# A fused encoder block on one core: seven-product jobs with a fourth raw buffer, splits placed where their target comes free, and wide closing weights

## The chip, the cores and the metric

The kernel runs on one core of one Trainium2 chip. The metric is the device time of one execution in microseconds (us). Engines are named as in the profile: PE is TensorE's matmul, PEld its weight load, DVE is VectorE, ACT is ScalarE, POOL is GpSimd, SP is the sync engine, which issues nearly all DMAs here.

## The reference

The program computes one block of an encoder over 512 frames of 1024 channels: a SwiGLU feed-forward, a mixer of two parallel branches, a second SwiGLU feed-forward, and a final normalisation.

```
def swiglu(h, w_in, w_out):
    a, b = jnp.split(h @ w_in, 2, axis=-1)
    return (jax.nn.silu(a) * b) @ w_out
...
    mod = (jax.nn.silu(c) @ w_ada[l] + b_ada[l]).reshape(B, 3, 3, 1024)
    h = modulate(rms_norm(x, g_ffn1[l]), mod[:, 0, 0], mod[:, 0, 1])
    x = x + 0.5 * mod[:, 0, 2][:, None, :] * swiglu(h, w_ffn1_in[l], w_ffn1_out[l])
    ...                                   # mixer: pooling branch and state-space branch
    h = modulate(rms_norm(x, g_ffn2[l]), mod[:, 2, 0], mod[:, 2, 1])
    x = x + 0.5 * mod[:, 2, 2][:, None, :] * swiglu(h, w_ffn2_in[l], w_ffn2_out[l])
return rms_norm(x, g_final)
```

The change lies in the second feed-forward: w_in is 1024 x 5632, w_out is 2816 x 1024. The 2816 gated channels are 22 blocks of 128, called f; the 1024 output channels are 8 blocks, called d.

## The kernel before

**Numbers as two halves.** All arithmetic is near full float32 precision: a matrix is split into a high half (a cast to the matmul's type, on ScalarE) and a low half (value minus high, a subtraction on VectorE). `put_split` (L262, L263) does this for activations, `split` (L1263, L1265) for weights. A product is then three matmuls: high x high, high x low, low x high (`mm3`, L257 to L259).

**Units.** The program is a list of units. A unit is one piece of weights (`src`), the matmuls that use it (`mm`), what comes before them (`pre`) and after them (`post`). One loop walks the list and issues everything; each engine then runs its own instructions in the order issued. Just before a unit's matmuls the loop calls `prefetch`, which issues splits and loads of later units: at position q, first all splits in `splits_at[q]`, then all loads in `loads_at[q]`. A plain unit is loaded 4 positions ahead (LA) into one of three `raw` buffers and split 2 ahead (SA) into one of three pairs of `wh` and `wl`. Units marked `late` prefetch behind their matmuls.

**The second feed-forward** (`ffn_seven`). In order:
- Eight steps, here g0 to g7, of the opening group (`group6`): step k multiplies 768 columns of weights with rows k of the normalised input, into six PSUM banks. The steps' `pre` also make the input: `make_h` for step k+1 (VectorE L215, ScalarE L219, VectorE L247, and on GpSimd an unsplit copy in HF, L221). When two steps' rows are there, `h_sums` forms four sums on GpSimd (L239 to L242), into two alternating 1024-column parts of MISC, and appends their split to `late_splits`. From k=4 on each `pre` first issues one of these. After g7, three gate stores (`gate_store`: silu, product, split).
- Two plain units, which give block f=3 (24 wide matmuls each; a third gate store pair's `post` issues late splits that are left).
- 36 jobs, numbered here 0 to 35, which give f=4 to 21. A job is a half of an inner dimension, computed as a seven-product scheme on 2 x 2 blocks of 256 frames. Jobs 4n and 4n+1 make the silu side of a pair of f's, 4n+2 and 4n+3 the other side. Each job has two units, here called 5a and 5b. The first unit (`mm1`) uses four weight blocks in `wh`/`wl`, 24 matmuls of 256 columns; the second (`mm2`) three blocks in one of four places of its own (J2A, J2A, J2B, and the second halves of HH and HL in even rows), 18 matmuls. After the first unit of an odd job `post1` forms sums of products inside PSUM: a copy on ScalarE (L547), four sums on VectorE (L548 to L551), a copy on ScalarE (L552). After the second unit of an odd job follows silu (`done_a`) or the gate product with its split (`done_b`).
- A job's four raw blocks are loaded into one of three raw buffers (two halves of MISC, and ADA); GpSimd then forms four more from them (L515 to L517). Both splits read the buffer. Order of units: 0a 1a, 2a 3a, 0b 1b, 4a 5a, 2b 3b, and so on.
- Outward units: three blocks of eight, each one d and six f's (18 wide matmuls), stand behind 4b 5b, 16b 17b and 28b 29b; the next job pair's first units follow. At the end the last four f's: four units of two f's ahead of and behind 34b 35b, four more of two f's, two of four f's, each with the residual, and the last two d's in `tail`, which runs them by halves of the frames so that the final norm can begin.
- `residual` (L634) adds to X on VectorE; for the last blocks ScalarE squares (L185) and scales (L646), and GpSimd adds the squares (L186).

Of the kernel before, what the change touches and what calls it, by code (L numbers as in the profile page):

```python
# [54 lines left out]
def block_kernel(ctx, tc, a, out):  # L55
# [175 lines left out]
    def h_sums(kp):  # L231
# [3 lines left out]
        o = 1024 * (kp % 2)  # L235
        t = MISC[:, o:o + 1024].rearrange("p (s t) -> p s t", s=4)
# [35 lines left out]
    def group6(s, src, post, pre0=None):  # L272
# [15 lines left out]
        for k in range(KT):  # L288
            def pre(k=k):
# [160 lines left out]
    def ffn_seven(s, w6, win, wout):  # L450


        JR = [MISC[:, 2048:4096], ADA, MISC[:, 0:2048]]
# [6 lines left out]
        def post6(pst):  # L460
            new_gslots()
            t1 = big("J2A", [P, 4096], F32R, "TB")
            t2 = big("J2B", [P, 2048], F32R, "MM")
            st8["p2"] = [(by256(t[:, o:o + 768]), by256(t[:, o + 768:o + 1536])) for t, o in ((t1, 0), (t1, 1536), (t2, 0))]

            st8["p2"].append((HH[:, 0:6:2, HB], HL[:, 0:6:2, HB]))
# [5 lines left out]
        def plain(f, ab, slot, hold):  # L472
# [13 lines left out]
            return Unit(win[ab], 1024, mm, None, post)  # L486
# [17 lines left out]
        def half_units(src, pr, kh, far):  # L504
# [3 lines left out]
            def load():  # L508
                t = JR[njob[0] % 3]
                job["n"], job["t"] = njob[0], t  # L510
                assert njob[0] < 3 or njob[0] - 3 in st8["free"]
                njob[0] += 1
                nc.sync.dma_start(out=t[:, 768:1792], in_=src)
                c = t.rearrange("p (i w) -> p i w", w=256)
# [4 lines left out]
            def split1():  # L519
# [24 lines left out]
            def post1():  # L544
                h1, h2 = slice(0, 256), slice(256, 512)
                e = ev()
                S.copy(out=e[:, h1], in_=pr.a[:, h1])  # L547
                V.tensor_tensor(out=e[:, h2], in0=pr.a[:, h2], in1=e[:, h1], op=ALU.add)  # L548
                V.tensor_tensor(out=e[:, h1], in0=pr.b[:, h1], in1=e[:, h2], op=ALU.add)
                V.tensor_tensor(out=pr.a[:, h2], in0=pr.b[:, h2], in1=e[:, h2], op=ALU.add)  # L550
                V.tensor_tensor(out=pr.b[:, h2], in0=pr.b[:, h2], in1=e[:, h1], op=ALU.add)  # L551
                S.copy(out=pr.b[:, h1], in_=e[:, h1])  # L552
# [11 lines left out]
            u1.load, u1.split, u1.lead, u1.far = load, split1, 3, far  # L564
            u2 = Unit(src, 768, mm2, None, pr.done if kh else None)
            u2.load, u2.split, u2.twin = (lambda: None), split2, u1
            return u1, u2

        def pair(n, slot):
# [10 lines left out]
            def done_b():  # L580
                two = lambda x: x.rearrange("p (f t) -> p f t", f=2)
                t, o, ol = (GHA, slot, GLA) if slot < 4 else (gslots["gc"], 0, None)
                for e, p, cs in zip(pa.s, (pb.a, pb.b), (HA, HB)):
                    g = ev()
                    V.tensor_tensor(out=g, in0=e, in1=p, op=ALU.mult)
# [4 lines left out]
                    put_split(hi, lo, two(g))  # L590
# [3 lines left out]
            for ab, pr in enumerate((pa, pb)):  # L594
                us = [half_units(win[2 + 4 * n + 2 * ab + kh], pr, kh, 6 if n else 4) for kh in range(2)]
# [3 lines left out]
        def out_unit(d, f0, f1, s0, hold, first=True, last=True, lastb=False):  # L599
            def mm(hi, lo):  # L600
                if first:
                    hold.append(ps())
                p = hold[0]
                for i in range(f1 - f0):
                    w = slice(i * P, (i + 1) * P)
                    mm3(p, hi[:, w], lo[:, w], *gslots[s0 + i], first and i == 0, last and i == f1 - f0 - 1)

            post = (lambda: residual(s, d, hold[0], lastb)) if last else None
            return Unit(wout[d, :, f0 * P:f1 * P], (f1 - f0) * P, mm, None, post)
# [8 lines left out]
        hold = [[] for _ in range(4)]  # L618
        for i in range(18):
# [612 lines left out]
    ffn_seven(2, a["w_f2_6"], a["w_f2_in"], a["w_f2_out"])  # L1232
# [5 lines left out]
    loads_at, splits_at = {}, {}  # L1238
    for j, i in enumerate(wunits):
        loads_at.setdefault(j - units[i].far, []).append(j)  # L1240
        t = units[i].twin
        splits_at.setdefault(j - units[i].lead if t is None else order[units.index(t)] - 1, []).append(j)
# [194 lines left out]
```

## Time and profile before

| | |
|---|---|
| median of 3 runs | 1090.03 us (1087.83 to 1090.41) |
| the profiled execution | 1087.91 us, span 1086.1 us, mean clock 0.987 |
| busy: PE, PEld | 1039.0 us (96%), 876.0 us (81%) |
| busy: DVE, ACT, POOL | 716.9 us (66%), 388.6 us (36%), 386.6 us (36%) |
| HBM | 126 GB/s over the span |

Rows of the profile read as follows. A timeline row has start, duration, engine, line, operation, output<-inputs, shapes, and in brackets the idle time before it with what ended it. Consecutive matmuls overlap, so their pace is read from start to start. A row of the waits has the total, the number and the longest. In rows of a list, three durations in ns are minimum, median and maximum; L263, for instance, is a helper's line and stands for all callers. The second feed-forward begins at about 690 us and runs to the end.

### The profile page before, as it was taken

To read this page: it belongs to the slowest core of one execution; us is meant where nothing else is said; L and a number is where in the kernel's file an instruction comes from. 1 tells how busy PE (TensorE), PEld (TensorE's weight loads), DVE (VectorE), ACT (ScalarE), POOL (GpSimd) and SP (SyncE) were. 2 spreads that over 40 slices of the span, in tenths; PEclk is the share of its full clock that TensorE was granted. 3 is DMA by queue.
4 is the path that set the end of the run, shared out by engine and by line. 5 is a ranking of instruction groups with operands and counts; after the bars stand their busy time and mean duration, and the time that the engine had idled before them with its cause. 6 is when DMAs were issued, how large, how long until landed. Compare 5 with 4: busy or idle time off the path is not lost.

```text
span 1086.1 us, 14290 instructions
## 1 busy us (share of the span) xinstructions
PE 1039.0 (96%) x5474; PEld 876.0 (81%) x5474; DVE 716.9 (66%) x1123; ACT 388.6 (36%) x589; POOL 386.6 (36%) x339
## 2 busy tenths in 40 slices
PE   9899999999999999989999999998999999999995
PEld 7678888888888888877888888977879888988874
DVE  6956878999796366789623474566636764675544
ACT  5242222222223243633343342344423542443343
POOL 2400100499885231234400001684433613562103
PEclk9999999999999999999999999998999999999998
DMA  9555554564474222222343322132232232323012
GB/s 351 196 208 199 196 194 159 203 220 168 165 243 177 65 80 77 94 68 78 105 137 107 97 97 83 44 101 84 84 131 78 79 126 87 99 102 132 35 54 88
DMA packets 46904, 138.24 MB, mean 127 GB/s; under 512 B 5218, under 2 KB 10466, under 8 KB 46835
## 3 DMA queue, kind: packets, MB, share of 16 engines
q1 hardware_dynamic: 46658, 136.73, 37.1%
q8 instruction: 43, 0.70, 0.3%
q0 software_dynamic: 176, 0.59, 0.1%
q14 instruction: 27, 0.21, 0.1%
HBM read 134.15 MB, written 3.15 MB: 126 GB/s over the span
## 4 chain that ended last, share of the span: by engine, by line
PE 68%; DVE 16%; ACT 5%; issue 4%; DMA 4%; POOL 2%; SPq 0%; DVEq 0%; ACTq 0%; POOLq 0%
PE ps L257 19%; PE ps L259 19%; PE ps L258 19%; PE ps L499 3%; DMA MISC<-w_f_in 2%; PE ps L282 2%; PE ps L283 1%; ACT wh L262 1%; PE ps L286 1%; DVE wl L1265 1%; DVE ev L693 1%; DVE J2A L263 1%; DVE ev L215 1%; DMA ADA<-w_f_in 1%; ACT wh L1263 1%
## 5 line engine op out<-in xcount | busy, mean ns | idle before, releaser
L1265 DVE TENSOR_TENSOR wl<-raw,wh 128x1024 fp32r<-128x1024 f32 (+4 forms) x157 | 182.3, 1167 | 89.5 <-ACT wh L1263 89.2
L259 PE MATMUL ps<-HH,wl 128*128 128x512 f32 (+1 forms) x544 | 212.0, 390 | 4.6 <-DVE wl L1265 4.6
L1263 ACT CAST wh<-raw 128x1024 fp32r<-128x1024 f32 (+4 forms) x171 | 151.3, 892 | 178.8 <-PE ps L258 88.2
L257 PE MATMUL ps<-HH,wh 128*128 128x512 f32 (+1 forms) x544 | 212.5, 391 | 0.0
L258 PE MATMUL ps<-HL,wh 128*128 128x512 f32 (+1 forms) x544 | 211.9, 389 | 0.0
L259 PEld LDWEIGHTS ps<-HH,wl 128*128 128x128 f32 x544 | 102.4, 188 | 29.0 <-DVE wl L1265 5.4
L257 PE MATMUL ps<-GHA,wh 128*128 128x512 f32 (+1 forms) x308 | 119.7, 389 | 6.1 <-ACT wh L1263 6.1
L257 PEld LDWEIGHTS ps<-HH,wh 128*128 128x128 f32 x544 | 102.4, 188 | 23.6 <-ACT PM L926 0.2
L258 PEld LDWEIGHTS ps<-HL,wh 128*128 128x128 f32 x544 | 102.3, 188 | 23.2
L259 PE MATMUL ps<-GHA,wl 128*128 128x512 f32 (+1 forms) x308 | 118.9, 386 | 1.2 <-DVE wl L1265 1.2
L258 PE MATMUL ps<-GLA,wh 128*128 128x512 f32 (+1 forms) x308 | 118.0, 383 | 0.0
L186 POOL TENSOR_TENSOR ACC<-ACC,ev 128x512 f32<-128x512 f32 x15 | 19.4, 1294 | 219.4 <-ACT ev L185 219.4
L634 DVE SCALAR_TENSOR_TENSOR X<-ps,MOD,X 128x512 f32<-128x512 f32 (+1 forms) x78 | 54.9, 705 | 61.1 <-PE ps L259 61.0
L515 POOL TENSOR_TENSOR MISC<-MISC 128x512 f32<-128x512 f32 x24 | 31.4, 1309 | 138.9 <-DMA MISC<-w_f_in 138.9
L132 DVE CUSTOM_DVE_ANT_0 ADA<-ADA,C,COL 128x1024 f32<-128x1024 f32 x50 | 74.8, 1496 | 0.0
L257 PEld LDWEIGHTS ps<-GHA,wh 128*128 128x128 f32 x308 | 57.8, 188 | 20.9 <-ACT wh L1263 8.8
L282 PE MATMUL ps<-HH,wh 128*128 128x512 f32 (+1 forms) x180 | 62.8, 363 | 8.8 <-ACT HH L219 8.8
L259 PEld LDWEIGHTS ps<-GHA,wl 128*128 128x128 f32 x308 | 57.8, 188 | 16.5 <-DVE wl L1265 4.1
L258 PEld LDWEIGHTS ps<-GLA,wh 128*128 128x128 f32 x308 | 57.8, 188 | 12.2 <-DVE GLA L263 0.2
L262 ACT CAST GHA<-ev 128x512 fp32r<-128x512 f32 x36 | 22.3, 621 | 121.3 <-DVE ev L406 76.3
L283 PE MATMUL ps<-HH,wl 128*128 128x512 f32 (+1 forms) x180 | 61.6, 356 | 0.5 <-DVE wl L1265 0.5
L499 PE MATMUL ps<-SH,wl 128*128 128x256 f32 x216 | 61.2, 283 | 0.0
(254 smaller groups left out, 2199.3 us busy)
## 6 DMA issues: line engine op xcount, KB each, us to landing
ADA<-w_ada SPq DMA_DIRECT2D x50, 512.0 KB, 3.6
raw<-w_f_in SPq DMA_DIRECT2D x40, 512.0 KB, 4.5
raw<-w_f_out SPq DMA_DIRECT2D x40, 384.0 KB, 3.6
MISC<-w_f_in SPq DMA_DIRECT2D x24, 512.0 KB, 3.5
raw<-w_in SPq DMA_DIRECT2D x18, 512.0 KB, 3.5
raw<-w_f SPq DMA_DIRECT2D x16, 384.0 KB, 3.7
ADA<-w_f_in SPq DMA_DIRECT2D x12, 512.0 KB, 3.5
raw<-w_f_out SPq DMA_DIRECT2D x16, 320.0 KB, 3.0
```

What stands on the lines that cost most here:

```text
L132: V.tensor_tensor_reduce(out=t, in0=t, in1=C, scale=1.0, scalar=bada[:, n:n + 1], op0=ALU.mult, op1=ALU.add, accum_out=MOD[:, n:n + 1],)
L257: E.matmul(pst, wh, xh, start=first, stop=False)
L258: E.matmul(pst, wh, xl, start=False, stop=False)
L259: E.matmul(pst, wl, xh, start=False, stop=last)
L262: S.copy(out=hi, in_=src)
L282: E.matmul(pst[m][:, cs], hi[:, w], xh, start=first, stop=False)
L283: E.matmul(pst[m][:, cs], lo[:, w], xh, start=False, stop=False)
L499: E.matmul(out_, w_[:, i, w], x_, start=first and n == 0, stop=last and n == 2, skip_group_check=True)
L515: G.tensor_tensor(out=c[:, 1:3], in0=c[:, 4:7:2], in1=c[:, 3:5], op=ALU.subtract)
L634: V.scalar_tensor_tensor(out=X[:, d, cs], in0=p[:, cs], scalar=MOD[:, s * 24 + 16 + d:s * 24 + 17 + d], in1=X[:, d, cs], op0=ALU.mult, op1 ...
L1263: S.copy(out=hi[:, 0:u.cols], in_=t)
L1265: eng.tensor_tensor(out=lo[:, 0:u.cols], in0=t, in1=hi[:, 0:u.cols].bitcast(F32), op=ALU.subtract)
```

## The change

- A fourth raw buffer: job n uses part n mod 4 of (first half of MISC, second half of MISC, MM, ADA). The sums of `h_sums` now go to four places in TB. The second units' four places are now TB, TB, the halves of HH and HL, and TB with C.
- Split and load positions are computed: a first unit or plain unit is split one position behind the third `wh` user before it, at most 4 ahead; a second unit one position behind the fourth second unit before it; a job is loaded where both splits of the job four before it are issued, jobs 0 to 3 at 7, 7, 7 and 5 positions ahead.
- The late splits leave the opening group and go, two each, to the `pre` of the two plain units.
- `post1`: all six instructions on VectorE. `done_b`: both products in place, then both casts, then both subtractions.
- The closing outward units, ten before, become three of 1024 columns (d 0 to 3 with f 18, 19; d 0 to 3 with f 20, 21; d 4, 5 with f 18 to 21), all behind 35b, with weights packed for them on the host.

Everything ahead of g3 is issued as before. The core of the diff:

```
@@ h_sums
-        o = 1024 * (kp % 2)
-        t = MISC[:, o:o + 1024].rearrange("p (s t) -> p s t", s=4)
+        t = TB.rearrange("p r q c -> p (r q c)")[:, 1024 * kp:1024 * kp + 1024].rearrange("p (s t) -> p s t", s=4)
@@ group6, pre
-                    if k >= 4 and late_splits:
-                        late_splits.pop(0)()
@@ plain
+            def pre():
+                for _ in range(2):
+                    late_splits.pop(0)()
             def post():
                 if ab:
                     gate_store(slot, hold[0], hold[1])
-                while late_splits:
-                    late_splits.pop(0)()
@@ half_units, load
-                t = JR[njob[0] % 3]
+                c = (MISC[:, 0:2048], MISC[:, 2048:4096], MM.rearrange("p q c -> p (q c)"), ADA)[n % 4]
@@ post1
-                S.copy(out=e[:, h1], in_=pr.a[:, h1])
-                V.tensor_tensor(out=e[:, h2], in0=pr.a[:, h2], in1=e[:, h1], op=ALU.add)
+                u2, u3 = e[:, h2], e[:, h1]
+                V.tensor_copy(out=u3, in_=pr.a[:, h1])
+                V.tensor_tensor(out=u2, in0=pr.a[:, h2], in1=u3, op=ALU.add)
...
-                S.copy(out=pr.b[:, h1], in_=e[:, h1])
+                V.tensor_copy(out=pr.b[:, h1], in_=u3)
@@ done_b
-                    g = ev()
-                    V.tensor_tensor(out=g, in0=e, in1=p, op=ALU.mult)
...
-                    put_split(hi, lo, two(g))
+                for e, p in zip(pa.s, (pb.a, pb.b)):
+                    V.tensor_tensor(out=e, in0=e, in1=p, op=ALU.mult)
+                for e, cs in zip(pa.s, (HA, HB)):
...
+                    S.copy(out=hi, in_=two(e))
+                    gs.append((hi, lo, two(e)))
+                for hi, lo, e in gs:
+                    V.tensor_tensor(out=lo, in0=e, in1=hi.bitcast(F32), op=ALU.subtract)
@@ end of ffn_seven
-        units.extend([out_unit(d, 18, 20, 0, hold[d], True, False) for d in range(2)])
         units.extend(seq[17][1])
-        units.extend([out_unit(d, 18, 20, 0, hold[d], True, False) for d in range(2, 4)])
-        units.extend([out_unit(d, 20, 22, 2, hold[d], False, True, True) for d in range(4)])
-        units.extend([out_unit(d, 18, 22, 0, [], lastb=True) for d in range(4, 6)])
+        hold = []
+        units.append(out_unit(range(4), 18, 20, 0, wend[0], hold, True, False))
+        units.append(out_unit(range(4), 20, 22, 2, wend[1], hold, False, True, True))
+        units.append(out_unit(range(4, 6), 18, 22, 0, wend[2], [], lastb=True))
@@ positions of splits and loads
-        loads_at.setdefault(j - units[i].far, []).append(j)
-        splits_at.setdefault(j - units[i].lead if t is None else order[units.index(t)] - 1, []).append(j)
+        if u.kind == 2:
+            split_at[j] = seconds[-4] + 1 if len(seconds) >= 4 else t - 1
...
+        split_at[j] = max(walls[-3] + 1, j - 4) if len(walls) >= 3 else j - SA
...
+            back = split_at[raws_of[-3]] if len(raws_of) >= 3 else -9
+            load_at[j] = max(split_at[j] - (3 if seconds else 2), back)
...
+        load_at[j] = max(split_at[seconds[n - 4]], split_at[jobs[n - 4]]) if n >= 4 else j - (7, 7, 7, 5)[n]
```

More of the change, by code (lines that the diff above doesn't have):

```diff
@@ L447, in ffn, with ffn_seven @@
         tail(s, wout[6, :, f0 * P:f1 * P], wout[7, :, f0 * P:f1 * P], f1 - f0, lambda k: gslots[k])
-    def ffn_seven(s, w6, win, wout):
-        JR = [MISC[:, 2048:4096], ADA, MISC[:, 0:2048]]
+    def ffn_seven(s, w6, win, wout, wend):
         st8 = {"free": set()}
@@ L461, in post6 @@
             new_gslots()
[L462 to L466, printed above, removed]
             for f in range(3):
@@ L502, in ffn_seven, with half_units @@
             pass
-        def half_units(src, pr, kh, far):
+        def half_units(src, pr, kh):
             job = {}
             def load():
-                t = JR[njob[0] % 3]
-                job["n"], job["t"] = njob[0], t
-                assert njob[0] < 3 or njob[0] - 3 in st8["free"]
+                n = njob[0]
+                assert n < 4 or n - 4 in st8["free"]
                 njob[0] += 1
-                nc.sync.dma_start(out=t[:, 768:1792], in_=src)
-                c = t.rearrange("p (i w) -> p i w", w=256)
+                c = (MISC[:, 0:2048], MISC[:, 2048:4096], MM.rearrange("p q c -> p (q c)"), ADA)[n % 4]
+                job["n"], job["t"] = n, by256(c)
+                nc.sync.dma_start(out=c[:, 768:1792], in_=src)
+                c = by256(c)
                 G.tensor_tensor(out=c[:, 1:3], in0=c[:, 4:7:2], in1=c[:, 3:5], op=ALU.subtract)
@@ L594, in pair, with out_unit, post @@
             for ab, pr in enumerate((pa, pb)):
-                us = [half_units(win[2 + 4 * n + 2 * ab + kh], pr, kh, 6 if n else 4) for kh in range(2)]
+                us = [half_units(win[2 + 4 * n + 2 * ab + kh], pr, kh) for kh in range(2)]
                 r.append(([u[0] for u in us], [u[1] for u in us]))
             return r
-        def out_unit(d, f0, f1, s0, hold, first=True, last=True, lastb=False):
+        def out_unit(ds, f0, f1, s0, src, hold, first=True, last=True, lastb=False):
+            nf = f1 - f0
             def mm(hi, lo):
                 if first:
[L602 to L609, printed above, removed]
+                    hold.extend(ps() for _ in ds)
+                for m, p in enumerate(hold):
+                    for i in range(nf):
+                        w = slice((m * nf + i) * P, (m * nf + i + 1) * P)
+                        mm3(p, hi[:, w], lo[:, w], *gslots[s0 + i], first and i == 0, last and i == nf - 1)
+            def post():
+                for d, p in zip(ds, hold):
+                    residual(s, d, p, lastb)
+            return Unit(src, len(ds) * nf * P, mm, None, post if last else None)
         hold = []
@@ L1236, in block_kernel @@
     order = {u: j for j, u in enumerate(wunits)}
-    loads_at, splits_at = {}, {}
-    for j, i in enumerate(wunits):
-        loads_at.setdefault(j - units[i].far, []).append(j)
-        t = units[i].twin
-        splits_at.setdefault(j - units[i].lead if t is None else order[units.index(t)] - 1, []).append(j)
+    wu = [units[i] for i in wunits]
+    split_at, load_at = {}, {}
+    walls, raws_of, jobs, seconds = [], [], [], []
+    for j, u in enumerate(wu):
+        if u.kind == 2:
+            t = wu.index(u.twin)
+            split_at[j] = seconds[-4] + 1 if len(seconds) >= 4 else t - 1
+            load_at[t] = load_at.get(t)
+            seconds.append(j)
+            continue
+        split_at[j] = max(walls[-3] + 1, j - 4) if len(walls) >= 3 else j - SA
+        walls.append(j)
+        if u.kind == 1:
+            jobs.append(j)
+        else:
+            back = split_at[raws_of[-3]] if len(raws_of) >= 3 else -9
+            load_at[j] = max(split_at[j] - (3 if seconds else 2), back)
+            raws_of.append(j)
+    for n, j in enumerate(jobs):
+        load_at[j] = max(split_at[seconds[n - 4]], split_at[jobs[n - 4]]) if n >= 4 else j - (7, 7, 7, 5)[n]
+    splits_at, loads_at = {}, {}
+    for at, by in ((split_at, splits_at), (load_at, loads_at)):
+        for j in sorted(at):
+            by.setdefault(at[j], []).append(j)
     def load(j):
```

39 lines of the change are left out of this document (25 added, 14 removed).

## The prediction

> **What bounds the kernel now.** I read the page's busy times first, then TensorE's waits, then its timeline through the last third, then the other engines at the places where TensorE stood still.
>
> ```profile
> span 1086.1 us, 14290 instructions
> PE 1039.0 (96%) x5474; PEld 876.0 (81%) x5474; DVE 716.9 (66%) x1123; ACT 388.6 (36%) x589; POOL 386.6 (36%) x339
> ```
>
> TensorE is the bound: 47 us of 1086 without a matmul. Its waits name who ends those gaps (total, times, longest):
>
> ```profile
> PE ps L499 <- DVE wl L263: 7.3, 9, 1.6
> PE ps L257 <- ACT wh L1263: 6.1, 6, 1.4
> ```
>
> Operands come late: the low halves of job weights (L263), the outward weights (L1263), and in the opening group the normalised rows (L219, the second row below). Idle time understates this, for matmuls after a gap can be slow, so I count from the starts of units. TensorE rows: first matmul of g4; of g6; of the first plain unit; of job unit 0a, and the one behind it; of the second outward unit of each of the three blocks; of the closing unit for d=6; and the sums of squares near the end.
>
> ```profile
> 709.87 0.40 PE L282 MATMUL ps<-HH,wh 128*128 128x512 f32 x1
> 721.14 0.50 PE L282 MATMUL ps<-HH,wh 128*128 128x512 f32 x1 [1.84 <-ACT HH L219]
> 731.18 0.40 PE L257 MATMUL ps<-HH,wh 128*128 128x512 f32 x1
> 742.38 0.28 PE L499 MATMUL ps<-HH,wh 128*128 128x256 f32 x1
> 742.50 0.28 PE L499 MATMUL ps<-HL,wh 128*128 128x256 f32 x1
> 792.66 0.40 PE L257 MATMUL ps<-GHA,wh 128*128 128x512 f32 x1
> 891.40 0.40 PE L257 MATMUL ps<-GHA,wh 128*128 128x512 f32 x1
> 990.03 0.40 PE L257 MATMUL ps<-GHA,wh 128*128 128x512 f32 x1
> 1064.05 0.39 PE L257 MATMUL ps<-GHA,wh 128*128 128x256 f32 x1
> 1071.95 0.58 PE L196 MATMUL ps<-ONE,ACC 128*128 128x1 f32 x4 [1.02 <-DVE ACC L352]
> ```
>
> The two plain units, 48 matmuls of 512 columns, take 11.20 us: 0.233 each without a gap. One of 256 takes half, 0.117. A first unit has 24 of these (2.8 us), a second unit 18 (2.1), an outward unit of six blocks 18 wide ones (4.2), a step of the opening group 18 wide ones (4.2). Taken minus ideal is what TensorE loses:
> - g4 to g7: 21.3 minus 4 x 4.2 = 4.5 us.
> - 742.38 to 792.66: 50.3 minus (eight first units, six second units, one outward unit) 39.2 = 11.1.
> - to 891.40: 98.7 minus (twelve first, twelve second, eight outward) 92.4 = 6.3. To 990.03: 98.6, the same work, 6.2.
> - to 1064.05: 74.0 minus (seven outward, four first, six second units, 72 wide matmuls at the end) 70.0 = 4.0.
> - to 1071.95: 7.9 minus 36 narrow matmuls, 4.2 = 3.7.
>
> Together 35.8 us; the change touches nothing ahead of g3 that runs. The gaps themselves (3a starts at 753.70, 0b at 759.82):
>
> ```profile
> 753.70 0.58 PE L499 MATMUL ps<-HH,wh 128*128 128x256 f32 x1 [2.76 <-ACT wh L262]
> 759.82 0.41 PE L499 MATMUL ps<-HH,J2A 128*128 128x256 f32 x1
> 864.17 0.39 PE L499 MATMUL ps<-HH,wl 128*128 128x256 f32 x1 [1.61 <-DVE wl L263]
> 886.59 0.50 PE L257 MATMUL ps<-GHA,wh 128*128 128x512 f32 x1 [1.09 <-ACT wh L1263]
> ```
>
> **The opening group.** Steps g4 to g7 each carry one late split (L242's sums). VectorE makes the next h and the split in one queue:
>
> ```profile
> 712.32 0.47 DVE L215 SCALAR_TENSOR_TENSOR ev<-X,GS,ps 128x256 f32<-128x256 f32 x1
> 716.84 1.76 DVE L263 TENSOR_TENSOR SL<-MISC,SH 128x1024 fp32r<-128x1024 f32 x1
> 718.52 0.47 DVE L215 SCALAR_TENSOR_TENSOR ev<-X,GS,ps 128x256 f32<-128x256 f32 x1
> ```
>
> From h to h 6.2 us, of which 1.7 is the split; without it 4.5, and TensorE needs 4.2. h of g6 and g7 then comes just in time: I book the whole 4.5 us. What is late next is GpSimd: the loads of jobs 0, 1, 2 now stand at g3 to g5, so their subtractions queue ahead of later HF copies and h_sums, and the scratch buffers (ev) wait for those copies. Gain if this bites: 2 us or so less.
>
> **The first jobs.** Prices, from the list of MISC's instructions (min/median/max ns):
>
> ```profile
> L515 POOL TENSOR_TENSOR MISC<-MISC x24: 1266/1296/1514, 730.8 to 1022.8; 128x512 f32<-128x512 f32 x24
> L516 POOL TENSOR_TENSOR MISC<-MISC x24: 724/744/1614, 732.1 to 1024.1; 128x256 f32<-128x256 f32 x24
> L262 ACT CAST wh<-MISC x24: 1042/1048/1063, 733.8 to 1026.9; 128x1024 fp32r<-128x1024 f32 x24
> L263 DVE TENSOR_TENSOR wl<-MISC,wh x24: 1209/1226/2039, 734.9 to 1027.9; 128x1024 fp32r<-128x1024 f32 x24
> L263 DVE TENSOR_TENSOR J2A<-MISC,J2A x12: 945/948/1497, 745.9 to 1020.3; 128x768 fp32r<-128x768 f32 x12
> DMA to landing us min/median/max: 2.2/3.5/5.2
> ```
>
> A job's raw block thus needs 3.5 us to land and 2.8 us on GpSimd (1.3 + 2 x 0.75); then ScalarE 1.05 and VectorE 1.2. The 2.76 us gap at 3a is this chain run bare, since job 3 reuses job 0's buffer:
>
> ```profile
> 746.96 0.33 SPq L513 DMA_DIRECT2D MISC<-w_f_in  x1
> 750.50 1.27 POOL L515 TENSOR_TENSOR MISC<-MISC 128x512 f32<-128x512 f32 x1 [7.65 <-DMA MISC<-w_f_in]
> ```
>
> With four buffers job 3 loads into ADA as soon as h_sums has read it: by my walk 732.6, landed 736, ready 739, ten us before use. (GpSimd has no gap from the end of the second h_sums at 709.8 on: eight HF copies, two h_sums of four, three jobs, 7.4 + 6.6 + 8.4 = 22.4.)
>
> ```profile
> 709.09 0.74 POOL L242 TENSOR_TENSOR MISC<-ADA,MISC 128x256 f32<-128x256 f32 x1
> 714.35 0.93 POOL L221 TENSOR_SCALAR C<-ev,MOD 128x256 f32<-128x256 f32 x1 [0.33 <-DVE ev L215]
> 738.01 0.59 ACT L404 ACTIVATE ev<-ps 128x512 f32<-128x512 f32 x1
> 740.18 0.59 ACT L404 ACTIVATE ev<-ps 128x512 f32<-128x512 f32 x1
> ```
>
> The sync queue has nothing urgent behind that wait (jobs 4 and 5 need job 0's and 1's splits). Job 4 loads at 740.7 and is ready at 746.9, for use at 754.
>
> The walk on ScalarE and VectorE starts at 726.7 (plain units, 4.5 earlier): three gate stores, 2.2 each (the last two rows), to 732.7; then four late splits and 0a, 1a, 0b back to back on VectorE at some 1.15, to 740.6; the gate store of slot 3; then 2a, ready about 744.2. TensorE wants 2a at 743.5 (737.9 plus two first units). So the moved late splits do cost something here: 0.5 us by medians, and if six of those VectorE instructions run at their maximum (2.0 for 1.2), 2 to 3 us, possibly with a slow stretch of matmuls. I take 2.5. After 2a nothing is late: 3a 746.2 for 746.8, product sums 749.4 for 749.6, 4a 750.6 for 754, 6a 757 for 763, first outward unit split two units before use. Of 11.1 us, 0.5 stays in the second units (they took 2.15 instead of 2.1 wherever nothing was late) and 2.5 is the new stall: gain 8.1.
>
> **The later stretches.** The 1.61 us gap is the same chain: 16a's raw block waits for 13's splits. Now loads stand five or more units ahead and the cast four units ahead, where the target is free. In steady work, four jobs are 19.6 us of TensorE. VectorE: 4 x (1.2 + 0.95), two product sums, one gate pair. Product sums before:
>
> ```profile
> 756.56 0.42 DVE L548 TENSOR_TENSOR ev<-ps,ev 128x256 f32<-128x256 f32 x1
> 758.21 0.38 ACT L552 COPY ps<-ev 128x256 f32<-128x256 f32 x1 [2.83 <-DVE ps L551]
> ```
>
> ScalarE stood 2.83 us for the last copy, behind which the next weight casts waited; that is the gap at 886.59, together with a split only two units ahead. Now six instructions on VectorE, 2.4 us. The two copies do not appear on VectorE in this trace: 0.42 is the sum beside them, bounds 0.2 and 0.8, that is 7 us less to 14 us more VectorE time over 18 product sums, hidden while VectorE has slack. The gate pair as two products and two subtractions of 0.7 each (near the 128x512 residual's 0.74, below) is 2.8. Sum 8.6 + 4.8 + 2.8 = 16.2 of 19.6. With the measured stretching (VectorE between 921 and 985, next row) 45.7 plus 5 for six pairs of copies is 51 in the 59 us that the stretch would then last: 86%, still not the bound.
>
> ```profile
> 692.00:742.00 50.00, 45.95 (x235) 38.31 (x236) 34.93 (x49) 23.15 (x35) 43.95 (x41) 0.97 0.27 84
> 921.00:985.00 64.00, 60.68 (x504) 59.57 (x502) 45.73 (x58) 27.45 (x43) 32.50 (x27) 1.00 0.28 93
> ```
>
> (Columns: stretch, length, busy TensorE, weight loads, VectorE, ScalarE, GpSimd, clock, DMA.) Walking a cycle in order, each first unit is split about 6 us before use and product sums are ready 7 us before the second unit. Gains: 6.3 - 0.7 = 5.6 and 6.2 - 0.7 = 5.5.
>
> **The end.** Outward units of one d each cost 3.3 us of a ring between VectorE and ScalarE, whatever TensorE needs:
>
> ```profile
> 1064.64 0.74 DVE L634 SCALAR_TENSOR_TENSOR X<-ps,MOD,X 128x512 f32<-128x512 f32 x1
> 1065.42 0.63 ACT L185 ACTIVATE ev<-X 128x512 f32<-128x512 f32 x1 [1.42 <-DVE X L634]
> 1069.51 1.31 POOL L186 TENSOR_TENSOR ACC<-ACC,ev 128x512 f32<-128x512 f32 x1 [2.05 <-ACT ev L185]
> ```
>
> Three wide units of 24 matmuls (5.6 us each) have all weights split before 34b. 35b's gate pair (2.8) hides under the first. Four residuals follow each other at 1.4 us, as the columns of the second finish; ScalarE's square and scaling fit in 1.4 each, GpSimd's add 1.31 too. By this the last add ends 2.7 us into the d=6 unit (now 6.8), and the sums of squares wait for TensorE's own 4.2 us. Gains: 4.0 - 0.3 = 3.7 and 3.5. The 14 us behind are unchanged.
>
> Sum: 4.5 + 8.1 + 5.6 + 5.5 + 3.7 + 3.5 = 30.9. The profiled execution took 1087.9 (span 1086.1), 0.2% below the median of 1090.03; 1087.9 - 30.9 = **1057.0**, which I forecast also for the median (1059 from the median itself).
>
> **Two rules beside the rows.** Behind the gap of 2.76 us the first matmul lasted 0.58 instead of 0.28, and 3a took 6.1 us in place of 2.8; after 1.84 us at 721.14, the clock in 692 to 742 reads 0.97. After 1.61 none was slow. The Trainium skill (TensorE: Matmul & The Clock Gate, Part 1) has the clock halved after an idle window of some 3.4 us; these rows show it after shorter gaps. If by that rule gaps this short cost no clock, the slow matmuls would have another cause and stay: 31 less the 3.3 us of 3a, an estimate of 28 us gained.
>
> VectorE subtractions in the list above range from 1.2 to 2.0, with GpSimd at work. The Trainium skill (SBUF — State Buffer, Who interferes with whom) says that a VectorE instruction with two SBUF inputs and a GpSimd one reading SBUF exclude each other, the later one blocked entirely. This speaks against denser work, and is the second rival.
>
> **Rivals.**
> - The first jobs stall more (20%): GpSimd was busy 44 of 50 us in 692 to 742 and now gets three jobs more before the sums; VectorE's walk slips by 3 to 6 us with slow matmuls. 1060 to 1063. For: the row. Against: the sums are needed only 6 us after GpSimd has them.
> - VectorE or GpSimd bounds the job stretches (10%). If each of eight subtractions in four jobs takes its maximum, 0.8 and 0.55 more, VectorE needs 16.2 + 5.4 = 21.6 against 19.9; 1.7 us over nine cycles, 15 us: 1072. Against: medians at the minimum.
> - The later stalls do not go, as splits moved ahead only wait elsewhere (8%): half of 11.1 stays: 1063.
> - Slower (2%): VectorE's product sums on the path of every second unit. It decides from 23.3 us of VectorE per four jobs, 30.9 / 9 more than TensorE's 19.9, or 7.1 above my sum; all its instructions would have to stretch by 44%. At 60%, 26 us, 6 x 9 = 54 us: 1111.
>
> **Numbers.** Forecast 60%, own range 1052 (every stall gone and no new one at 2a) to 1060. The range 1052 to 1066 adds the first and third rivals and leaves out the rest. Within 0.3% counts as no change (the runs spread 0.24%): faster 0.96, same 0.02, slower 0.02.
>
> **What would show it.** g4 to g7 at 4.2 us a step; no gap at 3a; a small one at 2a, ended by VectorE's wl; no gap ahead of outward units; squares' adds on GpSimd about 1.4 us apart. Wrong would be: TensorE waiting on VectorE's ps or wl throughout, or VectorE over 90% in the job stretches.

## The result and the profile after

The changed kernel takes 1061.32 us (median of 4 runs, 1060.37 to 1061.99), the kernel before beside it 1088.93 (1087.01 to 1090.41): a ratio of 0.9747, 95% interval 0.9726 to 0.9767. Faster, as forecast, by 27.6 us where 31 were expected: 1057.0 was forecast, in a range of 1052 to 1066. The profiled execution took 1061.94 us.

The span and the busy times on the page of the changed kernel, and its TensorE waits (total, times, longest):

```profile
span 1059.9 us, 14235 instructions
PE 1025.5 (97%) x5474; PEld 870.2 (82%) x5474; DVE 750.5 (71%) x1152; ACT 377.6 (36%) x546; POOL 405.7 (38%) x339
```

```profile
PE ps L281 <- ACT HH L219: 5.9, 7, 1.1
PE ps L492 <- DVE wl L262: 3.1, 3, 1.4
PE ps L492 <- ACT wh L261: 1.3, 2, 1.1
```

The wait for outward weights is gone, the one for low halves of job weights has gone from nine times to three. The starts of the same units as before, in TensorE's timeline (g4; first plain unit; 0a; second outward unit of each block; the d=6 unit; sums of squares), with every wait over 0.7 us of the stretch between:

```profile
709.07 0.39 PE L281 MATMUL ps<-HH,wh 128*128 128x512 f32 x1
725.95 0.40 PE L256 MATMUL ps<-HH,wh 128*128 128x512 f32 x1
738.41 0.39 PE L492 MATMUL ps<-HH,wh 128*128 128x256 f32 x1 [1.10 <-ACT wh L261]
740.27 0.39 PE L492 MATMUL ps<-HH,wl 128*128 128x256 f32 x1 [1.35 <-DVE wl L262]
745.86 0.39 PE L492 MATMUL ps<-HH,wl 128*128 128x256 f32 x1 [0.96 <-DVE wl L262]
750.19 0.38 PE L492 MATMUL ps<-HH,wl 128*128 128x256 f32 x1 [0.75 <-DVE wl L262]
784.88 0.40 PE L256 MATMUL ps<-GHA,wh 128*128 128x512 f32 x1
877.94 0.40 PE L256 MATMUL ps<-GHA,wh 128*128 128x512 f32 x1
971.00 0.40 PE L256 MATMUL ps<-GHA,wh 128*128 128x512 f32 x1
1041.31 0.28 PE L256 MATMUL ps<-GHA,wh 128*128 128x256 f32 x1
1045.93 0.58 PE L196 MATMUL ps<-ONE,ACC 128*128 128x1 f32 x4 [0.23 <-DVE ACC L349]
```

Differences of these starts, against those of before:

| stretch | before | after | gain | booked |
|---|---|---|---|---|
| g4 to the first plain unit | 21.3 | 16.9 | 4.4 | 4.5 |
| from there to the second outward unit of block 1 | 61.5 | 58.9 | 2.6 | 8.1 |
| to that of block 2 | 98.7 | 93.1 | 5.7 | 5.6 |
| to that of block 3 | 98.6 | 93.1 | 5.6 | 5.5 |
| to the d=6 unit | 74.0 | 70.3 | 3.7 | 3.7 |
| to the sums of squares | 7.9 | 4.6 | 3.3 | 3.5 |

Together 25.2 of the span's 26.2; 0.8 lies ahead of g4, where both kernels issue the same up to g3, and 0.2 behind. Five of six terms came out within 0.2 us. The first jobs missed by 5.5: from the first plain unit to 0b TensorE lost 8.3 us (1.26, 3.06, 1.86, 1.15, 0.68 and 0.31 in the second plain unit, 0a, 1a, 2a, 3a and 0b), where a stall of 2.5 was booked.

What VectorE and GpSimd did there, from their timelines: the first two gate products, a late split and the low half of 1a; on GpSimd, the first subtraction of job 2, the HF copies ahead of the second product, and job 3's three subtractions; and on ScalarE the first silu.

```profile
727.01 0.69 DVE L403 TENSOR_TENSOR ev<-ev,ps 128x512 f32<-128x512 f32 x1 [0.85 <-POOL ADA L221]
732.02 0.69 DVE L403 TENSOR_TENSOR ev<-ev,ps 128x512 f32<-128x512 f32 x1 [2.35 <-POOL ADA L221]
742.38 1.75 DVE L262 TENSOR_TENSOR SL<-TB,SH 128x1024 fp32r<-128x1024 f32 x1
744.05 1.75 DVE L262 TENSOR_TENSOR wl<-MISC,wh 128x1024 fp32r<-128x1024 f32 x1
```

```profile
727.82 1.30 POOL L510 TENSOR_TENSOR MM<-MM 128x512 f32<-128x512 f32 x1
731.07 1.82 POOL L221 TENSOR_SCALAR ADA<-ev,MOD 128x256 f32<-128x256 f32 x2
739.71 1.66 POOL L510 TENSOR_TENSOR ADA<-ADA 128x512 f32<-128x512 f32 x1 [3.44 <-DMA ADA<-w_f_in]
741.45 1.60 POOL L511 TENSOR_TENSOR ADA<-ADA 128x256 f32<-128x256 f32 x1
743.12 1.60 POOL L512 TENSOR_TENSOR ADA<-ADA 128x256 f32<-128x256 f32 x1
```

```profile
726.32 0.60 ACT L401 ACTIVATE ev<-ps 128x512 f32<-128x512 f32 x1
```

Two things are late. The second gate product stands 2.35 us for a scratch buffer that HF copies on GpSimd still read, and those are queued behind the forming of jobs. (The first one's 0.85 us are put down to the same, but its silu, too, ended only at 726.92, so the buffer cost nothing there.) And while GpSimd forms jobs, subtractions take 1.75 on VectorE (1.2 otherwise) and 1.60 on GpSimd (0.74 otherwise).

The rows also show how: the two engines take turns, and the recorded time of the later one holds its waiting. GpSimd's second subtraction ends at 743.05 and the late split at 744.13, 1.08 us behind it; GpSimd's third ends at 744.72, 0.59 behind that; the low half of 1a ends at 745.80, again 1.08 behind. In this trace, from 690 us on, all 21 VectorE subtractions of 1024 columns that start while a GpSimd instruction runs end 1.07 to 1.09 us behind its end, whether they took 1.36 or 2.32 us in all; the 11 during which a GpSimd instruction only starts take 1.21 to 1.23, as alone.

### The profile page after: what moved, and what is told of

Read it like the earlier page. It is cut to its first block, busy times and chain, and to the rows that moved or that the text cites. A ratio compares the mean times of both kernels' runs of the same rounds, so it can differ in the third digit from the quotient of the medians.

```text
span 1059.9 us, 14235 instructions
## 1 busy us (share of the span) xinstructions
PE 1025.5 (97%) x5474; PEld 870.2 (82%) x5474; DVE 750.5 (71%) x1152; ACT 377.6 (36%) x546; POOL 405.7 (38%) x339
## 4 chain that ended last, share of the span: by engine, by line
PE 82%; DVE 11%; POOL 2%; issue 1%; ACT 1%; DMA 1%; SPq 0%; DVEq 0%; ACTq 0%; POOLq 0%
PE ps L256 20%; PE ps L258 20%; PE ps L257 20%; PE ps L492 16%; PE ps L281 1%; PE ps L282 1%; DVE ev L705 1%; PE ps L285 1%; DVE U L997 1%; DVE ev L215 1%; DVE QM L132 1%; DVE TB L132 1%; DVE ACC L349 1%; DVE wl L1297 1%; PE ps L942 1%
## 5 line engine op out<-in xcount | busy, mean ns | idle before, releaser
L1297 DVE TENSOR_TENSOR wl<-raw,wh 128x1024 fp32r<-128x1024 f32 (+3 forms) x150 | 186.0, 1244 | 78.3 <-ACT wh L1295 78.1
L1295 ACT CAST wh<-raw 128x1024 fp32r<-128x1024 f32 (+3 forms) x164 | 150.4, 922 | 185.5 <-PE ps L257 99.9
L186 POOL TENSOR_TENSOR ACC<-ACC,ev 128x512 f32<-128x512 f32 x15 | 19.4, 1296 | 246.8 <-ACT ev L185 246.7
L492 PE MATMUL ps<-SL,wh 128*128 128x256 f32 x216 | 60.7, 281 | 0.0
L492 PE MATMUL ps<-SH,wh 128*128 128x256 f32 x216 | 60.7, 281 | 0.0
```

The source lines that it names most:

```text
L186: eng.tensor_tensor(out=acc[:, cs], in0=acc[:, cs], in1=sq[:, cs], op=ALU.add)
L492: E.matmul(out_, w_[:, i, w], x_, start=first and n == 0, stop=last and n == 2, skip_group_check=True)
L1295: S.copy(out=hi[:, 0:u.cols], in_=t)
L1297: eng.tensor_tensor(out=lo[:, 0:u.cols], in0=t, in1=hi[:, 0:u.cols].bitcast(F32), op=ALU.subtract)
```

## The experiments

Each edit is against the changed kernel. Theories at the start: A, the gate products wait for GpSimd's copies, so the order on GpSimd is at fault; P, the later stretches are won by the computed positions, not by the fourth buffer; and that single parts (splits moved, sums moved, wide units) are worth what was booked. Their rivals are named in the expectations; B there is that VectorE has too much work behind the opening group, whatever GpSimd does. C came later: GpSimd's forming of jobs 0 to 2 is at fault, wherever it stands in this stretch. The table has differences of starts, as above (from the sums of squares ahead of the opening group, 692.76 before and 691.98 after).

| kernel | median us (range) | ratio [95%] | norm to plain | to block 1 | to 2 | to 3 | to sums |
|---|---|---|---|---|---|---|---|
| before | 1088.93 | | 38.4 | 61.5 | 98.7 | 98.6 | 81.9 |
| after | 1061.32 (1060.37–1061.99) | 0.9747 [0.9726, 0.9767] | 34.0 | 58.9 | 93.1 | 93.1 | 74.9 |
| e1 | 1062.32 (1060.27–1062.67) | 0.9759 [0.9745, 0.9774] | 34.2 | 58.1 | 93.1 | 93.1 | 74.9 |
| e2 | 1061.87 (1061.12–1062.42) | 0.9758 [0.9744, 0.9773] | 37.1 | 55.7 | 93.1 | 93.1 | 74.9 |
| e8 | 1062.94 (1061.38–1064.18) | 0.9767 [0.9752, 0.9781] | 34.7 | 58.9 | 93.1 | 93.1 | 74.9 |
| e3 | 1066.72 (1065.85–1068.93) | 0.9807 [0.9791, 0.9822] | 41.4 | 56.1 | 93.1 | 93.1 | 74.9 |
| e9 | 1057.54 (1056.56–1058.33) | 0.9725 [0.9711, 0.9738] | 34.1 | 54.1 | 93.1 | 93.1 | 74.9 |
| e11 | 1057.93 (1057.05–1058.95) | 0.9730 [0.9716, 0.9743] | 34.1 | 54.0 | 93.1 | 93.1 | 74.9 |
| e12 | 1057.37 (1056.97–1057.86) | 0.9719 [0.9706, 0.9732] | 34.1 | 53.3 | 93.1 | 93.1 | 74.9 |
| e4 | 1063.62 (1062.83–1065.35) | 0.9773 [0.9756, 0.9789] | 35.8 | 58.4 | 93.1 | 93.1 | 74.9 |
| e5 | 1075.42 (1071.40–1076.62) | 0.9876 [0.9855, 0.9896] | 35.4 | 61.0 | 99.6 | 98.3 | 74.9 |
| e6 | 1062.65 (1061.49–1065.19) | 0.9761 [0.9745, 0.9778] | 34.4 | 59.1 | 93.1 | 93.1 | 74.9 |
| e10 | 1065.55 (1063.40–1069.05) | 0.9802 [0.9783, 0.9821] | 35.5 | 58.5 | 93.7 | 93.1 | 74.9 |
| e7 | 1068.53 (1067.55–1069.52) | 0.9819 [0.9804, 0.9834] | 34.0 | 59.0 | 93.1 | 93.1 | 80.8 |

**e1: jobs 1 and 2 loaded later**, so that GpSimd's copies come ahead of their subtractions.

```
-load_at[j] = ... if n >= 4 else j - (7, 7, 7, 5)[n]
+load_at[j] = ... if n >= 4 else j - (7, 5, 6, 5)[n]
```

> GpSimd's work for jobs 1, 2 and 3 moves behind the last h_sums (load positions 7, 5, 6, 5 ahead instead of 7, 7, 7, 5); nothing else changes. Theory A (the first jobs are late because the gate stores on VectorE wait for scratch buffers that GpSimd's HF copies still read, and these stand behind jobs 0 to 2 on GpSimd): VectorE's waits of 0.85 and 2.35 us for POOL L221 ahead of the gate products go, the loss of TensorE in the second plain unit and 0a (1.3 + 3.1 us in the changed kernel) falls under 1.5, that from 0a to 1b from 8 us to 3 to 5, and the time to 1056 to 1058. Rival B (four late splits between the gate stores and the first jobs' splits are simply too much work for VectorE and ScalarE): 0a's loss falls by 1 us at most, time 1060 to 1061.

The gate products no longer waited for GpSimd, yet the two stretches together lost as much (92.2 us for 92.9), and the time is above both forecasts. TensorE's two waits in 0a and 1a, then VectorE's late splits and the low half of 0a, then GpSimd beside them:

```profile
740.67 0.39 PE L492 MATMUL ps<-HH,wl 128*128 128x256 f32 x1 [1.90 <-DVE wl L262]
746.24 0.58 PE L492 MATMUL ps<-HH,wl 128*128 128x256 f32 x1 [2.50 <-DVE wl L262]
```

```profile
735.29 3.66 DVE L262 TENSOR_TENSOR SL<-TB,SH 128x1024 fp32r<-128x1024 f32 x2 [0.26 <-ACT SH L261]
738.87 1.74 DVE L262 TENSOR_TENSOR wl<-MISC,wh 128x1024 fp32r<-128x1024 f32 x1
740.53 3.98 DVE L262 TENSOR_TENSOR SL<-TB,SH 128x1024 fp32r<-128x1024 f32 x2
```

```profile
739.49 2.26 POOL L510 TENSOR_TENSOR ADA<-ADA 128x512 f32<-128x512 f32 x1
```

Two late splits in 3.66 and 3.98 us where 2.3 were walked: what the gate products gained, the splits lost, because the jobs' subtractions now ran beside them. Theory A fell.

**e2: the gate product in place of silu**, so that no second scratch buffer is needed. **e8: e1 and e2 together.**

```
-        g = ev()
-        V.tensor_tensor(out=g, in0=sl, in1=pb, op=ALU.mult)
-        put_split(*gslots[slot], g)
+        V.tensor_tensor(out=sl, in0=sl, in1=pb, op=ALU.mult)
+        put_split(*gslots[slot], sl)
```

> The gate stores form their product in place of the silu, so each takes one scratch buffer instead of two; GpSimd's order is that of the changed kernel. Theory A: the waits for POOL L221 ahead of the gate products go as well, though GpSimd is as late as before, and the last h_sums still ends at 736, so sums 2 and 3 are split no earlier than 737: TensorE's loss up to 1b falls from 8 to 4 to 6 us, time 1057 to 1059. Rival B: no change beyond 1 us, 1060 to 1062.

> Both GpSimd's order (jobs 1, 2 and 3 behind the last h_sums) and gate products in place, all else is the changed kernel. Theory A: either alone takes the scratch waits away, so both together equal the better one within 1 us, 1055 to 1058; what is left up to 1b (2 to 4 us) is ended by VectorE's wl and SL. Rival B: 1060 to 1061.

Neither gains: together the two stretches took 92.7 and 93.6 us. In e2 the first jobs lost 3.2 less, but the opening group as much more (waits of 0.54 and 0.27 for HH, which e5 and e10, without this edit, have too, and 1.3 more of slow matmuls right behind the norm, which e4 has too; that they come from the edit is not shown). In e8 nothing waits for a buffer, and two late splits take 4.00.

**e3: late splits back in the opening group.**

```
+                    if k >= 4 and late_splits:
+                        late_splits.pop(0)()
                     if k < KT - 1:
...
-                for _ in range(2):
+                while late_splits:
```

> The four late splits go back into the steps g4 to g7 of the opening group; all else is the changed kernel. Both theories: g4 to the first plain unit 21 us again instead of 16.9, which is 4.4 us more. Rival B (too much work after the group): the first jobs then lose 4 to 5 us less, time 1060 to 1062, the move is worth nothing. Theory A: the gate stores come 4 us later while GpSimd's list is the same length, so the scratch waits shrink too and the losses up to 1b fall under 3 us: time 1059 to 1061, the move as it was made is worth 0 or less, where the prediction booked 2 us.

TensorE's waits in the group return:

```profile
714.85 0.50 PE L281 MATMUL ps<-HH,wh 128*128 128x512 f32 x1 [1.40 <-ACT HH L219]
720.63 0.50 PE L281 MATMUL ps<-HH,wh 128*128 128x512 f32 x1 [1.31 <-ACT HH L219]
727.51 0.50 PE L281 MATMUL ps<-HH,wh 128*128 128x512 f32 x1 [2.41 <-ACT HH L219]
```

The group takes 7.4 us more, the first jobs 2.8 less: the move is worth 4.6 in the trace, 5.4 by the medians, where both theories had expected it to be worth nothing (1059 to 1062). The group loses more than the 4.4 that the change had gained there. Unlike in the kernel before, GpSimd forms jobs beside these splits; that this is the reason is not shown.

**e9: jobs 0 to 2 loaded 17 positions ahead**, beside the last outward units of the mixer. **e11: the same with e2.**

```
-load_at[j] = ... if n >= 4 else j - (7, 7, 7, 5)[n]
+load_at[j] = ... if n >= 4 else j - (17, 17, 17, 5)[n]
```

> Jobs 0, 1 and 2 are loaded and formed on GpSimd 17 positions ahead, beside the mixer's last outward units, where GpSimd is idle but for one 1.3 us add per 5.6 us; all else is the changed kernel, the number of instructions too. Theory C (GpSimd's subtractions and VectorE's subtractions from two SBUF inputs slow each other, so moving GpSimd's work within 700 to 750 us, as the first and the eighth experiment did, only moves the loss): the late splits on VectorE go from 1.75 to 2.3 us each to 1.2, no gate product waits for POOL, TensorE loses under 3 us from the plain units to 1b (8 now), time 1055 to 1057. Rival B (too many splits for VectorE, whatever GpSimd does): loss stays at 6 to 8, 1060 to 1062.

> Jobs 0 to 2 early as in the ninth experiment, and gate products in place. Theory C: with GpSimd's list short, scratch buffers are free in time anyway, so nothing beyond the ninth: within 1 us of it, 1054 to 1057. Rival A' (scratch buffers still hold the gate stores by a few tenths each): 1 to 2 us faster than the ninth. Rival B: 1060 to 1062.

The first jobs' stretch takes 54.1 instead of 58.9, and e9 is 3.8 us faster by the medians, its range clear of the changed kernel's. e11 is the same as e9: with the forming out of the way, the buffer is no longer waited for. GpSimd, VectorE and ScalarE of e9:

```profile
664.65 1.29 POOL L510 TENSOR_TENSOR MM<-MM 128x512 f32<-128x512 f32 x1 [1.03 <-DMA MM<-w_f_in]
```

```profile
738.27 2.34 DVE L262 TENSOR_TENSOR SL<-TB,SH 128x1024 fp32r<-128x1024 f32 x2
740.54 1.21 DVE L262 TENSOR_TENSOR wl<-MISC,wh 128x1024 fp32r<-128x1024 f32 x1
744.85 1.23 DVE L262 TENSOR_TENSOR wl<-MM,wh 128x1024 fp32r<-128x1024 f32 x1 [0.25 <-ACT wh L261]
```

```profile
743.25 0.62 ACT L261 CAST GHA<-ev 128x512 fp32r<-128x512 f32 x1 [1.27 <-DVE ev L403]
743.77 1.04 ACT L261 CAST wh<-MM 128x1024 fp32r<-128x1024 f32 x1
```

Now the third of these jobs is formed at 664.65, late splits and low halves take their 1.2 again, and the clock over 737 to 760 reads 1.00 in place of 0.93 (e9's row first, then that of the changed kernel):

```profile
737.00:760.00 23.00, 21.37 (x165) 19.92 (x164) 21.72 (x26) 13.27 (x17) 12.71 (x9) 1.00 0.27 93
```

```profile
737.00:760.00 23.00, 18.36 (x127) 16.71 (x126) 21.88 (x22) 13.20 (x16) 14.24 (x10) 0.93 0.28 92
```

The slow matmuls behind the 0.93 were no cause of the loss: in the changed kernel TensorE stood another 0.96 us for the low half of 1a behind them. Of the first jobs' loss 3.4 us are left, 1.4 of them at 2a: its cast (743.77) is queued on ScalarE behind the gate store of slot 3.

**e12: e9, and two of the four late splits ahead of the first plain unit.**

```
+                    for _ in range(2 if k == KT - 1 and late_splits else 0):
+                        late_splits.pop(0)()
...
-                for _ in range(2):
+                for _ in range(2 * ab):
```

> The ninth experiment's early jobs, and the first two late splits issued at the last step g7 of the opening group, where VectorE stands 2 us waiting for the group to end; the other two at the second plain unit. If what is left at 1a, 2a and 0b (2.6 us in the ninth) is the length of VectorE's queue behind the gate stores: two subtractions of 1.15 less in it, the gap at 2a goes, TensorE loses under 1.5 us from the plain units to 1b, 1055 to 1056.5. If instead the gate stores only start as much later: no change, 1057 to 1058.

No gain over e9 that can be told (1057.37 for 1057.54): the gap at 1a goes, and the waits at 2a stay, 0.21 and 0.76.

**e4: the product sums' two copies on ScalarE again.**

```
-                V.tensor_copy(out=u3, in_=pr.a[:, h1])
+                S.copy(out=u3, in_=pr.a[:, h1])
...
-                V.tensor_copy(out=pr.b[:, h1], in_=u3)
+                S.copy(out=pr.b[:, h1], in_=u3)
```

> The two copies of the product sums go back to ScalarE, the four sums stay on VectorE; all else is the changed kernel. Theory P (the positions of splits and loads carry the gain of the later stretches): ScalarE waits 2.8 us for each last copy again, but splits stand 4 units ahead, so no gap ahead of the outward blocks, 1060 to 1063. Rival Q (product sums on VectorE alone carry it): gaps of about 1 us ahead of each of the three outward blocks and waits for wl in the stretches return, 1065 to 1072.

The later stretches are those of the changed kernel to 0.1 us, and the first jobs' is 0.5 shorter. The profiled execution is 3.4 us longer (2.3 by the medians), where the edit issues nothing: 1.8 lie between norm and plain units, with the clock halved for 3.41 us right behind the norm, and 1.7 ahead of the norm. That the move of the copies gains anything is not shown by any stretch; where the 1.7 come from stays open.

**e5: three raw buffers**, the rest of the change kept (ADA left out, a job loaded behind the splits of the third before it).

```
-c = (MISC[:, 0:2048], MISC[:, 2048:4096], MM..., ADA)[n % 4]
+c = (MISC[:, 0:2048], MISC[:, 2048:4096], MM...)[n % 3]
...
-load_at[j] = max(split_at[seconds[n - 4]], split_at[jobs[n - 4]]) if n >= 4 else ...
+load_at[j] = max(split_at[seconds[n - 3]], split_at[jobs[n - 3]]) if n >= 3 else ...
```

> Three raw buffers instead of four (the two halves of MISC, and MM), a job loaded where the splits of the job three before it are issued; positions of splits, product sums, late splits and the closing units are those of the changed kernel. Theory P2 (in the later stretches the computed split positions are enough, the fourth buffer is needed for job 3 alone): the later stretches keep TensorE without a gap (under 1 us each beyond the changed kernel's), the first jobs lose 4 to 6 us more at 3a, time 1065 to 1068. Rival (the chain of load, GpSimd and split is what stalls 16a and 28a, and only the fourth buffer takes it away): 3 to 4 us come back in each of the two later stretches as well, time 1072 to 1076.

**e6: split and load positions of before**, four buffers kept. **e10: e6 and e4 together.**

```
-            split_at[j] = seconds[-4] + 1 if len(seconds) >= 4 else t - 1
+            split_at[j] = t - 1
...
-        split_at[j] = max(walls[-3] + 1, j - 4) if len(walls) >= 3 else j - SA
+        split_at[j] = j - (3 if u.kind == 1 else SA)
...
-            load_at[j] = max(split_at[j] - (3 if seconds else 2), back)
+            load_at[j] = j - LA
```

> Split and load positions of the kernel before (first units 3 ahead, others 2 ahead, second units one ahead of their job's first unit; plain loads 4 ahead) with the four raw buffers, product sums, late splits and closing units of the changed kernel. Theory P: gaps ahead of the three outward blocks return (about 1 us and 0.6 of slow matmuls each), and the wide closing units wait for their weights; time 1066 to 1070. Rival Q (four buffers with product sums on VectorE suffice): 1061 to 1063.

> Old positions of splits and loads and the copies of the product sums on ScalarE, both together, with four raw buffers, moved late splits and the wide end of the changed kernel. If either positions or copies is enough to close the gaps ahead of the outward blocks (each alone undone cost 2 us or less): about 1.7 us come back at each of the three blocks, 1067 to 1070. If the fourth buffer alone carries the later stretches: 1062 to 1065, no gap ahead of the second and third block.

These belong together. With three buffers the later stretches lose 6.5 and 5.2 us again, near all that the change had won there (5.7 and 5.6). With four buffers and the old positions they lose nothing, and with the copies on ScalarE too 0.6 and nothing. TensorE's waits in e5, one of each stretch, and on GpSimd the job that it waits for, standing for its load:

```profile
774.24 0.39 PE L492 MATMUL ps<-HH,wl 128*128 128x256 f32 x1 [1.55 <-DVE wl L262]
873.92 0.58 PE L492 MATMUL ps<-HH,wl 128*128 128x256 f32 x1 [1.65 <-DVE wl L262]
972.09 0.38 PE L492 MATMUL ps<-HH,wl 128*128 128x256 f32 x1 [1.56 <-DVE wl L262]
```

```profile
868.54 1.28 POOL L510 TENSOR_TENSOR MISC<-MISC 128x512 f32<-128x512 f32 x1 [2.91 <-DMA MISC<-w_f_in]
```

Theory P fell: without the fourth buffer the later stretches lose about what they had lost before, and with it they lose 0.6 us at most, whatever of positions and copies is undone. (The new order of `done_b` is in every run, so what it is worth is not shown.) In e5 the rival came, with more per stretch than its 3 to 4 us; the first jobs lost 2.1 us more, where 4 to 6 were expected at 3a. At block 1 the old positions cost 0.85 us in e6 and 0.95 in e10, waits for outward weights. (e10's median is 4.2 us above the changed kernel's with a spread of 5.7; its trace is 1.7 longer. Where the rest is, stays open.)

**e7: the ten narrow closing units.**

```
-        units.append(out_unit(range(4), 18, 20, 0, wend[0], hold, True, False))
-        units.append(out_unit(range(4), 20, 22, 2, wend[1], hold, False, True, True))
-        units.append(out_unit(range(4, 6), 18, 22, 0, wend[2], [], lastb=True))
+        units.extend([out_unit([d], 20, 22, 2, w2(d, 20, 22), hold[d], False, True, True) for d in range(4)])
+        ...
```

> The ten narrow closing outward units of the kernel before, all else is the changed kernel. The prediction's step: the 3.3 us ring of VectorE and ScalarE per unit returns, GpSimd's adds 3.3 us apart, 3.7 us more to the d=6 unit and 3.3 more to the sums of squares: 1068 to 1069. Rival (the computed positions alone, with weights split 4 ahead, take most of the ring away): under 1064.

7.2 us slower by the medians, 5.9 in the last column. The adds of squares on GpSimd come 3.3 us apart again, while in the changed kernel they end 3.1 us into the d=6 unit of 1041.31 (second fence):

```profile
1039.09 1.29 POOL L186 TENSOR_TENSOR ACC<-ACC,ev 128x512 f32<-128x512 f32 x1 [2.12 <-ACT ev L185]
1042.41 1.29 POOL L186 TENSOR_TENSOR ACC<-ACC,ev 128x512 f32<-128x512 f32 x1 [2.02 <-ACT ev L185]
```

```profile
1036.06 2.69 POOL L186 TENSOR_TENSOR ACC<-ACC,ev 128x512 f32<-128x512 f32 x2 [0.17 <-ACT ev L185]
1043.07 1.31 POOL L186 TENSOR_TENSOR ACC<-ACC,ev 128x512 f32<-128x512 f32 x1 [0.99 <-ACT ev L185]
```

## Why the prediction was right, and where it was not

**Right, and shown.** The opening group: 4.4 for 4.5, and e3 gives it back and more (7.4). The raw chain in the later stretches: 5.7 and 5.6 for 5.6 and 5.5, and e5 gives it back. The end: 7.0 for 7.2, ring and all, and e7 gives back 5.9 in its trace, 7.2 by the medians.

**The step that failed is the first jobs' term**, booked at 8.1 and measured at 2.6. The walk let the three gate stores end at 732.7; the third ended at 736.8. It had the late splits with 0a, 1a and 0b end at 740.6; they ended at 746.7. And 2a, walked to 744.2, was ready at 750.1. The prediction had seen both causes and left part of them out of its sum. The wait for HF copies was named at "2 us or so", which is what it came to (2.35), but it stands in no term. The stretched subtractions were priced at "2 to 3 us" for the late splits and the job halves, and these took 2.0 more (9.9 us up to 746.7, for 7.9 walked); the same stretching of the gate stores' own subtractions (1.28, 0.87 and 1.26 us for 0.69, 1.3 in all) was put at nothing. And the prediction set the second rival's rule against medians of the whole stretch ("medians at the minimum"), though GpSimd works there without a gap of more than 0.1 us up to 736.3, and forms job 3 from 739.7 to 744.7, beside the last splits (walked: ready at 739). The outcome is the first rival's (VectorE's walk slipping by 3 to 6 us with slow matmuls, 1060 to 1063): the time lies outside the forecast's own range of 1052 to 1060 and inside the stated one only because that rival had been added. That the gain of 27.6 us lies near the 28 given for slow matmuls that stay is chance: 3a, which carried those, takes 3.5 us now (752.88 to 756.36) for 6.1. e9 checks the walk itself: with the forming of jobs 0 to 2 taken away from this place, gate stores end at 734.4, 2a is ready at 746.1, TensorE loses 3.4 us against 2.5 booked, and the kernel takes 1057.5 against 1057.0.

What is shown: that GpSimd's forming beside VectorE's splits costs some 4 us (3.8 by the medians, 4.8 in the stretch), in whatever order (e1, e2, e8), and none of it when done earlier (e9). The Trainium skill (SBUF — State Buffer, Who interferes with whom) has a VectorE instruction with two SBUF inputs and a GpSimd one that reads SBUF contend for an exclusive lock. The traces agree: the later of the two ends a fixed time behind the earlier one (1.07 to 1.09 us for VectorE's 1024 columns, 21 of 21), where a slowdown of both would let the overlap set the time.

**A right sum with an attribution that is not shown.** The gap at 886.59, ahead of block 2, was put down to ScalarE's 2.83 us wait for the product sums' last copy and a split two units ahead. e6 has that split and e4 that copy, and neither loses anything on the way to block 2; e10, with both, loses 0.6. But e5, with three buffers and the new split, has no gap ahead of block 2 either: its 6.5 us come from waits of job units between 860 and 874 us. So that gap goes in more than one way, and no single cause of it is shown; what needs the fourth buffer is the job units. The 5.6 were right because they were counted as a whole.

**The margin was thinner than walked.** The copies took 0.41 and 0.43 us, as taken (0.42), but in the job stretch before block 3 VectorE is at 53.6 of 59.6 us, 90%, for the 86% walked, since with GpSimd denser more of them wait for the other engine, and the medians, which hold that waiting, moved. The window, and two rows of the list of MISC's instructions (before: 1296 and, for J2A, 948):

```profile
907.10:966.70 59.60, 59.60 (x506) 59.55 (x505) 53.62 (x68) 26.76 (x35) 41.99 (x32) 1.00 0.35 115
```

```profile
L510 POOL TENSOR_TENSOR MISC<-MISC x18: 1291/1750/2277, 711.5 to 956.8; 128x512 f32<-128x512 f32 x18
L262 DVE TENSOR_TENSOR J<-MISC,J x18: 947/1492/1655, 745.7 to 971.1; 128x768 fp32r<-128x768 f32 x18
```

TensorE has no gap there, so the second rival did not come; but a walk by medians from a trace in which the two engines meet less is a walk from below.

**Open.** The step at 2a: issuing its cast ahead of the gate store of slot 3 was not tried. The new order of `done_b` was not undone by itself. And kernels that issue the same up to the norm reach it between 690.6 (e5) and 694.1 us (e6), so a difference of 2 us between two medians of this table says little unless the stretch shows it.

## What to carry to other kernels

Book a stall by the stretch it is in, and attribute it only after one part at a time has been undone: here one more buffer kept two stretches free whichever of two other edits was undone. Before moving work to an engine that "has time", lay out who else is busy at that place: each GpSimd subtraction beside VectorE's made one of the two wait for the other, and the same work some 60 us earlier (664.65 for 727.82) cost nothing that a stretch shows. e9, one line beyond the change, and e12 are the fastest versions measured, the same within their ranges.

## What the runs showed of the hardware that was not expected

How long TensorE stood still at one gap did not by itself decide whether slow matmuls follow. Behind single gaps of 1.55 and 1.65 us in e5 (rows above), 17 and 14 matmuls took about 0.2 us for 0.117, and in the changed kernel 15 did behind 1.10 and 1.35 us; behind the gap of 1.90 in e1 and one of 2.20 in e8 none did, while behind the next ones, 2.50 in both, 13 did. The three gaps of before (none behind 1.61, slow behind 1.84 and 2.76) looked like a limit near 1.7 us; these runs show none there.

The granted clock in the traces shows what goes with it. In each of the fourteen, all its changes lie on one grid of 3.413 us, to 0.002 us, and within the second feed-forward it is halved for one step of the grid or two. Three such steps of the changed kernel (the clock is the third column from the right):

```profile
737.95:741.37 3.42, 1.60 (x11) 1.40 (x12) 3.42 (x3) 3.26 (x4) 1.66 (x1) 1.00 0.30 116
741.37:744.78 3.41, 3.41 (x17) 3.23 (x16) 3.41 (x3) 0.62 (x1) 3.20 (x2) 0.50 0.02 5
744.78:748.20 3.42, 2.46 (x21) 2.34 (x21) 2.73 (x4) 1.60 (x4) 0.00 (x0) 1.00 0.13 16
```

In the first TensorE stood 1.82 us, and the clock is halved in the next. So it is throughout: between 700 and 1040 us, the 12 steps at full clock in which TensorE stood 1.63 us or longer in all, 1.634 to 2.46, were each followed by one at half clock, and none with less was (the most is 1.630, in e1). At half clock less is enough: a step with 0.77 was followed by another one in the kernel before, one with 0.38 in e1 was not. A step boundary cuts the gap of 1.90 in e1 and that of 2.20 in e8, and leaves 1.63 and 1.49 in the worse step. So the same gap can cost a slow step or not, by where the grid lies. Outside this part idle time read in this way gives no single limit (1.13 was enough right behind the norm in e2 and e4, 1.76 was not at 463 us in e4), so it is not the whole rule. The Trainium skill (TensorE: Matmul & The Clock Gate, Part 1) names an idle window of some 3.4 us; the grid here has that step, but half of it idle was enough, and the measurements decide.
